# Regrouping positions by their residue of 16, and turning the dilation-16 probabilities with VectorE's 32x32 block transposes

## The chip, the core and the metric

One core of a Trainium2 chip runs the whole program in one launch. TensorE (PE; PEld is its weight load) does matmuls, VectorE (DVE) and ScalarE (ACT) the elementwise work, GpSimd (POOL) some elementwise work and the DMAs that add while they write, and SyncE (SP) issues most DMAs. The metric is the device time of one execution in microseconds, as the median of several runs.

## The reference

Two encoder layers work on 512 positions of width 1024 in float32. Each normalises x, projects it, runs two attention branches, gates both with SiLU, projects back and adds to x. Branch A is latent attention with 8 heads. Branch B is dilated attention in three groups (window, dilation): (128, 1), (512, 4) and (2048, 16), each with 8 heads of 64. Positions are gathered by stride, so that a query of group g sees only keys of its own residue class modulo the dilation:

```python
for g, (window, dil) in enumerate(DIL_PAIRS):
    ...
    o, lse = banded_attention(to_strided(q, dil), to_strided(k, dil), to_strided(v, dil),
                              window // (2 * dil))
...
alpha = jax.nn.softmax(jnp.stack(lses, axis=0), axis=0)
out = jnp.einsum('gbsh,gbshd->bshd', alpha, jnp.stack(outs, axis=0).astype(jnp.float32))
```

With 512 positions, dilation 16 has 16 classes of 32 positions, and the window of 2048 takes in each class whole. Dilation 4 has 4 classes of 128 positions and a band of 64 to either side. The three outputs of a position are weighted by their softmax denominators.

## The kernel before, in words

Activations lie with features on the 128 partitions and the 512 positions along the row. The positions do not lie in natural order: `order()` sorts them by residue of 4, so that each of the four residue classes is one block of 128 columns. Inside a block they are in ascending order. Heads are treated in pairs p = 0..3 (a = 0, 1 is the head of the pair, on 64 partitions each).

The dilated work is cut into 12 units u, each a group g and a pair p. Units 0, 1, 6, 7 have g = 0 (dilation 1, "near"), units 2, 3, 8, 9 have g = 1, and units 4, 5, 10, 11 have g = 2 (dilation 16). A unit makes q and k from a projection (`dil_qk`, which calls `rope`), then scores (`near_scores` or `far_scores`), then the product with the values (`near_out` or `far_out`).

- Near units need positions in another order than the rest, since a dilation of 1 crosses the four blocks. They are re-sorted on the way. `near_values` (L572) writes the values in chunks of 128 positions, `rope` does it for keys (L642) and for queries (L645, in two pieces of 128 and 384 columns), and `merge_rows` (L452, two pieces) puts the output back. All four are VectorE additions or products that have to run anyway. The re-sorting is in their access patterns, which have contiguous runs of 32 or 16 floats.
- The near units' running minima and sums (16 bytes per position) are re-sorted by DMAs through memory, in `by_residue`: one write (L702) and five reads (L706 to L708) per pair, on SP's queue.
- `far_scores` works per block of 128 positions for g = 1 and g = 2 alike: a 128x128 score block, a mask added by VectorE (L758), and a minimum taken by a custom instruction (L761); then ScalarE's exponential (L765). For g = 1 the mask is a band. For g = 2 it lets through a quarter of the block: keys that agree with the query modulo 4 within the block. For g = 2 the shares of the three groups follow (`shares`, L809 to L818), and POOL multiplies the probabilities by them (L773, 8 instructions of 128x128).
- `far_out` turns the probabilities, so that keys lie on partitions. `transpose_split` does it with four 128x128 transposes on TensorE into a PSUM bank (L457). ScalarE copies the bank as a rounded high part (`split`, L222), VectorE makes the low part (L223), and TensorE multiplies with the values (L793). ScalarE and VectorE add up the halves (L796, L797, L799).

Matmuls in full precision are made of three products of high and low parts, `triple` (L242 to L244). So weights are also split after loading: ScalarE copies the high part (L199), VectorE subtracts (L204), or POOL issues a DMA that adds (L202).

The order of the work is made by `Weave.run`. A main line of projections runs on, and side lines (norms, scores, outputs, combination) give pieces in between when their needs were finished a set lag ago. Each piece yields what it costs TensorE in this plan, and `LG2` is the lag between a dilation-16 unit's scores and its turning. Behind that a scheduler puts the instructions on each engine's queue, which then runs strictly in order.

## Time and profile before

| | |
|---|---|
| median of 3 runs | 933.5 us (932.68 to 936.16) |
| the profiled execution | 936.2 us |
| its span, first to last instruction | 934.4 us |
| PE busy | 910.4 us (97%) |
| DVE busy | 690.9 us (74%) |
| ACT busy | 597.8 us (64%) |
| POOL busy | 315.1 us (34%) |
| granted TensorE clock | 0.995 |

The profile is of one execution, which is 0.3% above the median. The matmuls' durations overlap (each row's mean is from its start to its modelled end), so what one of many costs is better read from the spacing of their starts. The chain of waits is followed back from the last instruction, and each of its pieces is time in which that instruction kept the end waiting. Time is in microseconds from the start of the span.

### The profile page before, as it was taken

The numbers are of one execution on the slowest core, as the hardware profiler recorded it, in microseconds if no ns is written. First come the engines' busy times: TensorE is split into PE (matmuls) and PEld (weight loads), VectorE is DVE, ScalarE is ACT, GpSimd is POOL, SyncE is SP. The second block draws the span as 40 slices with busy tenths as digits, with TensorE's granted clock in tenths as the row PEclk, the third lists the DMA queues.
The fourth block names the chain that finished last, engine by engine and source line by source line (L and its number), as shares of the span: only waits on it lengthen the run. The fifth ranks groups of instructions, "written<-read, shape, count | busy, mean of one in ns | idle before, by whom it ended". The sixth has DMA issues, their size and how long they took to land.

```text
span 934.4 us, 15835 instructions
## 1 busy us (share of the span) xinstructions
PE 910.4 (97%) x5172; PEld 775.1 (83%) x5172; DVE 690.9 (74%) x1732; ACT 597.8 (64%) x1448; POOL 315.1 (34%) x367
## 2 busy tenths in 40 slices
PE   8999999999999999999999999999999999999996
PEld 6978888988889889887897888888888888897775
DVE  6756787877868766688766578797778776757864
ACT  6546776666857766754454578666767586676533
POOL 0034253344542431333312444423554234224300
PEclk9999999999999999999999999999999999999999
DMA  7357453276554764655553854516666557366432
GB/s 272 115 121 141 105 122 68 66 161 147 122 123 93 149 131 104 136 147 147 171 155 104 163 121 86 114 46 138 139 129 148 131 101 148 84 144 144 130 123 90
DMA packets 85746, 118.66 MB, mean 127 GB/s; under 512 B 16864, under 2 KB 34848, under 8 KB 85664
## 3 DMA queue, kind: packets, MB, share of 16 engines
q1 hardware_dynamic: 65648, 81.80, 29.8%
q0 software_dynamic: 19584, 35.66, 24.2%
q8 instruction: 41, 0.67, 0.3%
q14 instruction: 41, 0.34, 0.1%
q10 hardware_dynamic: 432, 0.20, 0.1%
HBM read 113.26 MB, written 4.36 MB: 126 GB/s over the span
## 4 chain that ended last, share of the span: by engine, by line
PE 81%; DVE 8%; ACT 4%; DMA 3%; issue 3%; POOL 1%; ACTq 0%; DVEq 0%; POOLq 0%
PE bank L242 22%; PE bank L244 22%; PE bank L243 22%; PE bank L457 5%; PE bank L558 3%; PE bank L752 1%; PE bank L793 1%; PE bank L681 1%; DMA whl<-wst 1%; DVE pt L223 1%; DMA wraw<-wst 1%; ACT whl L199 1%; DVE tmp L638 1%; POOL tmp L636 1%; DVE whl L204 1%
## 5 line engine op out<-in xcount | busy, mean ns | idle before, releaser
L242 PE MATMUL bank<-hl,whl 128*128 128x512 f32 x728 | 290.2, 399 | 2.2 <-ACT hl L222 1.4
L244 PE MATMUL bank<-hl,whl 128*128 128x512 f32 x728 | 284.4, 391 | 2.0 <-DMA whl<-wst 2.0
L243 PE MATMUL bank<-hl,whl 128*128 128x512 f32 x728 | 284.5, 391 | 0.0
L199 ACT CAST whl<-wraw 128x512 fp32r<-128x512 f32 (+3 forms) x243 | 143.8, 596 | 119.4 <-PE bank L244 77.5
L202 POOL DMA_DIRECT2D whl<-wst x136 | 119.7, 889 | 223.9 <-ACT whl L201 161.5
L244 PEld LDWEIGHTS bank<-hl,whl 128*128 128x128 f32 x728 | 136.7, 188 | 32.5 <-DMA whl<-wst 2.9
L242 PEld LDWEIGHTS bank<-hl,whl 128*128 128x128 f32 x728 | 136.6, 188 | 29.2 <-ACT hl L222 1.8
L243 PEld LDWEIGHTS bank<-hl,whl 128*128 128x128 f32 x728 | 137.0, 188 | 24.6 <-DVE hl L223 0.3
L242 PE MATMUL bank<-whl,hl 128*128 128x256 f32 (+2 forms) x328 | 99.8, 304 | 1.5 <-ACT hl L222 1.5
L244 PE MATMUL bank<-whl,hl 128*128 128x256 f32 (+2 forms) x328 | 98.3, 300 | 0.0
L243 PE MATMUL bank<-whl,hl 128*128 128x256 f32 (+2 forms) x328 | 98.1, 299 | 0.0
L204 DVE TENSOR_TENSOR whl<-wraw,whl 128x512 fp32r<-128x512 f32 (+3 forms) x107 | 76.1, 717 | 26.0 <-ACT whl L199 25.0
L636 POOL TENSOR_TENSOR tmp<-tmp,sd 128x512 f32<-128x512 f32 x48 | 63.2, 1316 | 89.5 <-DVE tmp L634 65.4
L223 DVE TENSOR_TENSOR pt<-bank,pt 128x512 fp32r<-128x512 f32 x128 | 83.6, 684 | 5.6 <-ACT pt L222 4.2
L201 ACT ACTIVATE whl<-wraw 128x512 fp32r<-128x512 f32 x136 | 86.3, 635 | 0.1
L222 ACT CAST pt<-bank 128x512 fp32r<-128x512 f32 x128 | 69.9, 588 | 10.7 <-PE bank L457 10.3
L538 POOL TENSOR_SCALAR p<-p,lc 128x512 f32<-128x512 f32 x64 | 48.9, 771 | 71.4 <-DVE lc L537 70.6
L457 PE MATMUL bank<-ident,p 128*128 128x128 f32 x512 | 67.7, 275 | 0.0
L242 PEld LDWEIGHTS bank<-whl,hl 128*128 128x128 f32 x328 | 62.5, 191 | 3.9 <-ACT hl L222 1.8
L244 PEld LDWEIGHTS bank<-whl,hl 128*128 128x128 f32 x328 | 62.5, 191 | 2.0 <-DVE hl L223 0.4
L243 PEld LDWEIGHTS bank<-whl,hl 128*128 128x128 f32 x328 | 62.5, 191 | 1.7
L457 PEld LDWEIGHTS bank<-ident,p 128*128 128x128 f32 x512 | 59.2, 142 | 5.4
(178 smaller groups left out, 1612.5 us busy)
## 6 DMA issues: line engine op xcount, KB each, us to landing
wraw<-wst SPq DMA_DIRECT2D x218, 256.0 KB, 2.9
whl<-wst POOLq DMA_DIRECT2D x136, 256.0 KB, 4.5
tmp<-shd SPq DMA_DIRECT2D x32, 128.0 KB, 4.4
xl<-xT SPq DMA_DIRECT2D x10, 256.0 KB, 2.7
wraw<-wst SPq DMA_DIRECT2D x16, 144.0 KB, 2.2
wraw<-wst SPq DMA_DIRECT2D x12, 192.0 KB, 2.6
x1d<-xl SPq DMA_DIRECT2D x8, 256.0 KB, 2.9
xl<-x1d SPq DMA_DIRECT2D x8, 256.0 KB, 3.0
```

The lines of the kernel that those rows point to most:

```text
L199: nc.scalar.copy(hi, src)
L201: nc.scalar.mul(lo, src, -1.0)
L202: nc.gpsimd.dma_start(lo, wst[l * len(PLAN) + i, :, :c], accum_op=ALU.add)
L204: nc.vector.tensor_tensor(lo, src, F(hi), op=ALU.subtract)
L222: nc.scalar.copy(dst_hi, src)
L223: nc.vector.tensor_tensor(dst_lo, src, F(dst_hi), op=ALU.subtract)
L242: nc.tensor.matmul(a, w[:, 0], h[:, 0], start=first, stop=False)
L243: nc.tensor.matmul(a, w[:, 0], h[:, 1], start=False, stop=False)
L244: nc.tensor.matmul(a, w[:, 1], h[:, 0], start=False, stop=last)
L457: nc.tensor.transpose(b[:, 128 * i:128 * i + 128], x, ident)
L538: nc.gpsimd.tensor_scalar(pt, pt, l1, 0.0, op0=ALU.mult, op1=ALU.add)
L636: nc.gpsimd.tensor_tensor(u, u, L.sd, op=ALU.mult)
```

## The change

The positions inside each block of 128 get another order: first by residue of 16, then ascending. So a block is now four runs of 32 positions, one for each class of dilation 16, and a 128x128 block of dilation-16 probabilities has nonzero values only in its four 32x32 blocks on the diagonal. The mask for g = 2 changes with that, and so do the tables and the order in which x is handed over.

- In `far_out` with g = 2, VectorE's 32x32 block transpose (one instruction over the 128x512 tile, in place) stands where four TensorE transposes into a bank stood. ScalarE's copy and VectorE's subtraction now read the tile in place of the bank. The piece yields 0.0 in place of 0.9 to the weave.
- The re-sorting of the near units now goes between "block, residue of 16, ascending" and "ascending, residue". The access patterns of L572, L642, L645 and L452 take single floats at a step of 32 floats on one side; they had runs of 32 or 16 floats.
- `by_residue` writes with three DMAs (one of 128x3x4 floats, two of 64x4) in place of one, and reads with four in place of five.

```diff
-def near_chunks(x):
-    return x.rearrange("p (r c t) -> p c r t", r=4, c=4)
+def by_16(x):
+    return x.rearrange("p (m s) -> p s m", m=16)
...
     def near_values(L, p):
-        nc.vector.tensor_tensor(f.rearrange("p (c r t) -> p c r t", c=4, r=4), near_chunks(a), near_chunks(L.rb), op=ALU.mult)
+        nc.vector.tensor_tensor(f.rearrange("p (s m) -> p s m", m=16), by_16(a), by_16(L.rb), op=ALU.mult)
...
-    halfway = [(lambda f: f[:, 0:128].rearrange("p (r h t) -> p r h t", r=4, h=2),
-                lambda x: x.rearrange("p (r b t) -> p r b t", r=4, t=16)[:, :, 0:8:7]),
-               (lambda f: f[:, 128:512].rearrange("p (i r t) -> p r i t", i=3, r=4),
-                lambda x: x.rearrange("p (r t) -> p r t", r=4)[:, :, 16:112].rearrange("p r (i t) -> p r i t", i=3))]
+    halfway = [(lambda f: f[:, 0:128].rearrange("p (h s m) -> p h s m", h=2, m=16),
+                lambda x: x.rearrange("p (m b s) -> p b s m", m=16, s=4)[:, 0:8:7]),
+               (lambda f: f[:, 128:512].rearrange("p (s m) -> p s m", m=16), lambda x: by_16(x)[:, 4:28])]
...
         if order == "keys":
-            nc.vector.tensor_tensor(f.rearrange("p (c r t) -> p c r t", c=4, r=4), near_chunks(t1), near_chunks(u), op=ALU.add)
+            nc.vector.tensor_tensor(f.rearrange("p (s m) -> p s m", m=16), by_16(t1), by_16(u), op=ALU.add)
...
     def by_residue(L, p):
-        nc.sync.dma_start(sd.rearrange("(i m) x -> m i x", m=128), st)
+        nc.sync.dma_start(sd[64:448].rearrange("(i m) x -> m i x", m=128), st[:, 1:4])
+        for h in range(2):
+            nc.sync.dma_start(sd[448 * h:448 * h + 64], st[64 * h:64 * h + 64, 0])
         L.st[p] = t([128, 4, 3, 4], F32, "st", 4)
-        blocks = sd.rearrange("(i r t) x -> i t r x", i=4, r=4)
-        for i in range(3):
-            nc.sync.dma_start(L.st[p][16 + 32 * i:48 + 32 * i, :, 0], blocks[i + 1])
-        nc.sync.dma_start(L.st[p][0:16, :, 0], blocks[0, 0:16])
-        nc.sync.dma_start(L.st[p][112:128, :, 0], blocks[0, 16:32])
+        for m in range(4):
+            nc.sync.dma_start(L.st[p][32 * m:32 * m + 32, :, 0], sd.rearrange("(s r m) x -> m s r x", r=4, m=4)[m])
...
     def far_out(L, u):
             pt = L.p.pop(("d", u, rp))
-            tts.append(transpose_split([pt[:, 128 * i:128 * i + 128] for i in range(4)]))
+            if g == 2:
+                nc.vector.transpose(pt, pt)
+                tt = t([128, 2, S], FR, "pt", 2)
+                split(tt[:, 0], tt[:, 1], pt)
+                tts.append(tt)
+            else:
+                tts.append(transpose_split([pt[:, 128 * i:128 * i + 128] for i in range(4)]))
         yield ("t", L.l, "d", u)
-        yield 0.9, LG
+        yield 0.9 if g == 1 else 0.0, LG
...
 def order():
-    return np.arange(S).reshape(128, 4).T.reshape(-1)
+    return np.arange(S).reshape(32, 4, 4).transpose(2, 1, 0).reshape(-1)
```

What is left out are the masks and the tables that follow from the new order, and the shape of the mask in L758 (four rows of 32 in place of 32 rows of 4).

The scheduler places the new instructions by what they need, and not where the code stands. Three places matter below. The names carry buffer numbers, which differ between the two programs; lines from L703 on are up to 5 higher after the change.

The first place is VectorE's queue in layer 0, behind the shares of unit 10; `og` and its `tmp` belong to the unit before it, q and kst (with their `tmp`) to unit 11. Before:

```order
L797 TENSOR_TENSOR tmp_4700<-bank_4697,tmp_4700 64x2x128
L799 TENSOR_TENSOR og_4635<-bank_4697,tmp_4700 64x256
L223 TENSOR_TENSOR q_4674<-tmp_4668,q_4674 128x512
L223 TENSOR_TENSOR pt_4715<-bank_4710,pt_4715 128x512
L223 TENSOR_TENSOR pt_4723<-bank_4718,pt_4723 128x512
L634 STREAM_SHUFFLE tmp_4745<-bank_4684 128x512
L635 TENSOR_TENSOR tmp_4744<-bank_4684,cd_455 128x512
L638 TENSOR_TENSOR tmp_4744<-tmp_4744,tmp_4745 128x512
L223 TENSOR_TENSOR kst<-tmp_4744,kst 128x512
```

The same stretch after the change:

```order
L801 TENSOR_TENSOR tmp_4688<-bank_4685,tmp_4688 64x2x128
L781 STREAM_TRANSPOSE p_4556<-p_4556 128x512
L223 TENSOR_TENSOR q_4662<-tmp_4656,q_4662 128x512
L803 TENSOR_TENSOR og_4623<-bank_4685,tmp_4688 64x256
L223 TENSOR_TENSOR pt_4703<-bank_4698,pt_4703 128x512
L223 TENSOR_TENSOR pt_4711<-bank_4706,pt_4711 128x512
L633 STREAM_SHUFFLE tmp_4733<-bank_4672 128x512
L634 TENSOR_TENSOR tmp_4732<-bank_4672,cd_455 128x512
L781 STREAM_TRANSPOSE p_4583<-p_4583 128x512
L637 TENSOR_TENSOR tmp_4732<-tmp_4732,tmp_4733 128x512
L223 TENSOR_TENSOR kst<-tmp_4732,kst 128x512
```

The two transposes of unit 10 were put far ahead of the unit's output work. The first stands ahead of the low part of unit 11's q, the second between the two additions that make unit 11's k.

The second place is TensorE's queue where unit 10 was turned. Before, the turning stood between unit 11's scores and a projection:

```order
L755 MATMUL bank_4884<-kst,q_4674 128x128
L755 MATMUL bank_4885<-kst,q_4674 128x128
L457 MATMUL bank_4923<-ident,p_4568 128x128 x4
L457 MATMUL bank_4931<-ident,p_4595 128x128 x4
L242 MATMUL bank_4819<-hl_183,whl_4755 128x512
L243 MATMUL bank_4819<-hl_183,whl_4755 128x512
```

The same place after the change:

```order
L753 MATMUL bank_4872<-kst,q_4662 128x128
L753 MATMUL bank_4873<-kst,q_4662 128x128
L242 MATMUL bank_4807<-hl_183,whl_4743 128x512
L243 MATMUL bank_4807<-hl_183,whl_4743 128x512
L244 MATMUL bank_4807<-hl_183,whl_4743 128x512
```

The eight transposes are gone. All eight dilation-16 units of the two layers lose theirs, 64 in all, and the rest of TensorE's queue keeps its order but for five matmuls.

The third place is VectorE's queue at unit 10's low parts (`pt` from the turned probabilities). Before, they stood behind the minima of unit 11 (`p_4883`):

```order
L761 ISA p_4883,st_3966<-bank_4885,p_4883 128x128
L761 ISA st_3966 128x1
L223 TENSOR_TENSOR pt_4928<-bank_4923,pt_4928 128x512
L809 TENSOR_REDUCE mm_4904<-st_3966 128x8
L223 TENSOR_TENSOR pt_4936<-bank_4931,pt_4936 128x512
```

After, the first stands in front of a weight's low part (`whl`) and ahead of all of unit 11's minima (`p_4832` is its first half):

```order
L434 SCALAR_TENSOR_TENSOR gate_4786<-gate_4786,tmp_4784 128x512
L803 TENSOR_TENSOR og_4770<-bank_4789,tmp_4792 64x256
L223 TENSOR_TENSOR pt_4912<-p_4556,pt_4912 128x512
L204 TENSOR_TENSOR whl_4862<-wraw_4860,whl_4862 128x512
L756 TENSOR_TENSOR p_4832<-bank_4833,msk 128x2x128
L756 TENSOR_TENSOR p_4832<-bank_4834,msk 128x2x128
```

The second low part stands behind that first half of the minima, so both moved up on VectorE. In layer 1 the same three places look the same.

More of the change, by code (lines that the diff above doesn't have):

```diff
@@ L741, in far_scores @@
         st = L.st[p][:, :, g]
-        m = msk[:, 512:640].rearrange("p (x y) -> p x y", y=4) if g == 1 else msk[:, 640:644].unsqueeze(1).to_broadcast([128, 32, 4])
+        m = msk[:, 512:640].rearrange("p (x y) -> p x y", y=32) if g == 1 else msk[:, 640:644].unsqueeze(2).to_broadcast([128, 4, 32])
         pt = t([128, S], F32, "p", 8)
@@ L745, in far_scores @@
         banks = [bank() for _ in range(2)]
-        by4 = lambda x: x.rearrange("p j (x y) -> p j x y", y=4)
+        by4 = lambda x: x.rearrange("p j (x y) -> p j x y", y=32)
         for j in range(2):
@@ L757, in far_scores @@
             s = banks[a].rearrange("p (j l x) -> p j l x", j=2, l=2)
-            nc.vector.tensor_tensor(by4(p4[:, :, a]), by4(s[:, :, 0]), m.unsqueeze(1).to_broadcast([128, 2, 32, 4]), op=ALU.add)
+            nc.vector.tensor_tensor(by4(p4[:, :, a]), by4(s[:, :, 0]), m.unsqueeze(1).to_broadcast([128, 2, 4, 32]), op=ALU.add)
             for j in range(2):
@@ L1104, in constants @@
     tables = np.ascontiguousarray(np.stack([cd, sd, cmq, smq])[:, :, order()], np.float32)
-    near = np.arange(S).reshape(4, 32, 4).transpose(0, 2, 1).reshape(-1)
+    near = np.arange(S).reshape(32, 4, 4).transpose(0, 2, 1).reshape(-1)
     keytab = np.stack([c32, s32])[:, :, order()].reshape(2, 32, 4, 128).transpose(3, 0, 2, 1).reshape(128, 256)
@@ L1109, in constants @@
     q = near[:128, None] + 64
-    ends = np.where(near[:128, None] < 64, near[:128, None], 384 + near[:128, None])
-    i, j = np.arange(128)[:, None], np.arange(128)[None, :]
-    ok = [np.abs(q - k) <= 64, np.abs(ends - np.where(k < 128, k, 256 + k)) <= 64, np.abs(i - j) <= 64, i % 4 == j[:, :4]]
+    ends = np.concatenate([near[:64, None], near[448:, None]])
+    i = order()[:128] // 4
+    i, j = i[:, None], i[None, :]
+    ok = [np.abs(q - k) <= 64, np.abs(ends - np.where(k < 128, k, 256 + k)) <= 64, np.abs(i - j) <= 64, i % 4 == j[:, :128:32] % 4]
     masks = np.where(np.concatenate(ok, axis=1), 0.0, BIG).astype(np.float32)
```

## The prediction

> **What bounds the kernel now.** I read the page first, then the chain of waits, then single stretches of the timeline. The profiled execution took 936.2 us: a span of 934.4 and 1.8 around it.
>
> ```profile
> span 934.4 us, 15835 instructions
> PE 910.4 (97%) x5172; PEld 775.1 (83%) x5172; DVE 690.9 (74%) x1732; ACT 597.8 (64%) x1448; POOL 315.1 (34%) x367
> ...
> PE 81%; DVE 8%; ACT 4%; DMA 3%; issue 3%; POOL 1%; ACTq 0%; DVEq 0%; POOLq 0%
> ```
>
> TensorE is busy 97% of the span and carries 81% of the chain, so work taken off it shortens the run, except in the stretches where the chain runs through VectorE, ScalarE or a DMA. There TensorE would only wait longer. The chain shows three such stretches that lie on the changed units. At the end of layer 0, around unit 11's scores:
>
> ```profile
> 393.70 0.68 ACT p L765 x4
> ...
> 400.10 0.90 DVE q L223
> ...
> 422.77 0.73 PE bank L242 x2
> ```
>
> From 393.7 to 422.8 nearly every link is VectorE's, one instruction behind the other. At the end of layer 1 the chain comes in over a DMA instead, joins VectorE at 866.9, and later goes over weights:
>
> ```profile
> 857.25 6.15 DMA whl<-wst
> ...
> 866.95 0.69 DVE whl L204
> ...
> 873.10 0.60 DVE pt L223
> ...
> 878.94 0.50 PE bank L242
> ...
> 890.96 4.26 DMA wraw<-wst
> ...
> 904.30 0.47 PE bank L793 x2
> ```
>
> **TensorE's 64 transposes.** They lie in eight groups of eight, one for each dilation-16 unit. Where a group stands on the chain it costs 0.87 us, as in the first and the last of five such groups (units 4, 5 and 11 of layer 0, units 4 and 5 of layer 1):
>
> ```profile
> 234.52 0.88 PE bank L457 x8
> ...
> 738.99 0.87 PE bank L457 x8
> ```
>
> The other three lie in the stretches above, two beside unit 11's scores and one in the tail of layer 1:
>
> ```profile
> 412.96 1.09 PE L457 MATMUL bank<-ident,p 128*128 128x128 f32 x8
> 869.23 1.09 PE L457 MATMUL bank<-ident,p 128*128 128x128 f32 x8
> 892.83 1.03 PE L457 MATMUL bank<-ident,p 128*128 128x128 f32 x8
> ```
>
> All eight would give 8 x 0.87 = 7.0 us. I count the five on the chain, **-4.4 us**, and nothing for the three, since there TensorE waits for others at 422.8, 878.9 and 904.3. The bounds are -4.4 and -7.0. The mean of 275 ns that the by-form groups give for one of these transposes is not their price, because they overlap:
>
> ```profile
> L457 PE MATMUL bank<-ident,p 128*128 128x128 f32 x512 | 67.7, 275 | 0.0
> L634 DVE STREAM_SHUFFLE tmp<-bank 128x512 f32<-128x512 f32 x48 | 35.7, 744 | 0.1
> L223 DVE TENSOR_TENSOR pt<-bank,pt 128x512 fp32r<-128x512 f32 x128 | 83.6, 684 | 5.6 <-ACT pt L222 4.2
> ```
>
> **VectorE's 16 block transposes.** No row shows one. The nearest is the shuffle of a 128x512 tile, which also moves data across partitions: 744 ns. I take 0.75 us, so VectorE gains 16 x 0.75 = 12 us of work. The bounds are nothing (if they fit into idle time everywhere) and twice the row, 1.5 us. VectorE has 934.4 - 690.9 = 243 us idle, so what counts is where they land. In the five groups on TensorE's chain I cost them at nothing: VectorE's idle time and the plan's lags hide them, and if that cover were gone each pair would cost up to its 1.5 us. The first place is VectorE's queue of layer 0 at 399.6, with what GpSimd does at that time:
>
> ```profile
> 399.18 0.43 DVE L797 TENSOR_TENSOR tmp<-bank,tmp 64x256 f32<-64x256 f32 x1
> 399.64 0.43 DVE L799 TENSOR_TENSOR og<-bank,tmp 64x256 f32<-64x256 f32 x1
> 404.46 0.69 DVE L638 TENSOR_TENSOR tmp<-tmp,tmp 128x512 f32<-128x512 f32 x1 [0.92 <-POOL tmp L636]
> 398.35 3.59 POOL L773 TENSOR_SCALAR p<-p,e 128x128 f32<-128x128 f32 x8
> ```
>
> The first transpose needs GpSimd's first four share products, which end about half way through the eight, at 398.35 + 1.80 = 400.15. It comes up at 399.62, waits 0.5, runs 0.75, and q's low part, then k and everything behind them start 1.05 to 1.25 later; I take **+1.1 us**. The second comes where VectorE waits 0.92 us for GpSimd and fits. Were it 1.5 us long, both would cost 0.75 + 0.6 more. In layer 1 the same delay ends in the idle 0.83 us ahead of the weight at 866.95, since the chain there comes over the DMA:
>
> ```profile
> 866.95 0.69 DVE L204 TENSOR_TENSOR whl<-wraw,whl 128x512 fp32r<-128x512 f32 x1 [0.83 <-ACT whl L199]
> ```
>
> Unit 11's own transposes fall, in layer 0, between weight splits that wait for ScalarE and, in layer 1, into the 1.23 and 0.60 us shown here:
>
> ```profile
> 429.41 0.69 DVE L204 TENSOR_TENSOR hl<-wraw,hl 128x512 fp32r<-128x512 f32 x1 [0.76 <-ACT hl L199]
> 430.73 0.69 DVE L204 TENSOR_TENSOR hl<-wraw,hl 128x512 fp32r<-128x512 f32 x1 [0.63 <-ACT hl L199]
> 887.75 1.39 DVE L204 TENSOR_TENSOR whl<-wraw,whl 128x512 fp32r<-128x512 f32 x2 [1.23 <-ACT whl L199]
> 892.98 0.69 DVE L839 TENSOR_TENSOR og<-og,tmp 128x512 f32<-128x512 f32 x1 [0.60 <-DMA tmp<-shd]
> ```
>
> I cost them at nothing; at 1.5 us each they would overfill these gaps by about 1 us in each layer.
>
> **The low parts that move up.** The copy and the subtraction read the tile in place of a bank, at the same price, I assume: both engines handle such tiles all the time. In layer 1 the first low part moves into the 0.83 us at 866.1 and leaves the chain, where it stood with 0.60 at 873.10: **-0.6 us**. In layer 0 there is no gap at its new place, and nothing is won. Bounds: 0 and -1.2.
>
> **The re-sorting at a step of 32 floats.** It touches VectorE only. These are the groups, each for all eight near units (L645 and L452 have a second piece of 128 columns, and L452 runs once for each head):
>
> ```profile
> L642 DVE TENSOR_TENSOR tmp<-tmp,tmp 128x512 f32<-128x512 f32 x8 | 5.5, 689 | 4.2 <-POOL tmp L636 4.2
> L572 DVE TENSOR_TENSOR tmp<-bank,rb 128x512 f32<-128x512 f32 x8 | 5.5, 684 | 3.8 <-PE bank L244 3.8
> L452 DVE TENSOR_TENSOR og<-bank,tmp 64x384 f32<-64x384 f32 x16 | 8.8, 547 | 0.0
> L452 DVE TENSOR_TENSOR og<-bank,tmp 64x128 f32<-64x128 f32 x16 | 4.6, 287 | 4.4 <-ACT tmp L450 4.3
> ```
>
> So five passes over 512 columns for a near unit: one for values, one for keys, one for queries, two for outputs. They run at (547 - 287)/256 = 1.02 ns per column, with runs of 16 to 32 floats. The trace has no wide operation at a step above one float. The nearest rows are two tiny reductions over 24 floats: L809 steps by four floats, L816 by two.
>
> ```profile
> L809 DVE TENSOR_REDUCE mm<-st 128x8 f32<-128x24 f32 x8 | 1.4, 177 | 0.1
> L816 DVE TENSOR_REDUCE ls<-el 128x8 f32<-128x24 f32 x8 | 1.3, 166 | 0.0
> ```
>
> The wider step costs 11 ns for 24 floats, 0.46 ns per float, so 0.23 us for a pass of 512. The bounds are 0 and a doubled pass, 0.52. On the chain stand six of these passes, the first and the last being:
>
> ```profile
> 93.50 0.68 DVE tmp L642
> ...
> 587.30 0.77 DVE og L452 x2
> ```
>
> 6 x 0.23 = **+1.4 us**, between 0 and 3.1. The other 34 passes lie beside TensorE's work and add 34 x 0.23 = 8 us to VectorE's; without that cover they would count in full.
>
> **The sums' DMAs and the weave.** A pair issues three writes and four reads in place of one and five. I cost this at nothing. The reads go out when all writes have landed, as before with one, and SP's weight loads queue behind them; the consumers come a unit later. If a write landed a microsecond late, the weights behind it would, eight times in the run. The mask keeps its number of elements.
>
> **The sum**: -4.4 + 1.1 - 0.6 + 1.4 = **-2.5 us**. That makes 936.2 - 2.5 = 933.7 for the profiled execution, and 933.5 - 2.5 = **931.0** for the median.
>
> **Rivals.** *Everything comes through* (faster). All eight groups count, the block transposes and the steps cost nothing on the path: -7.0 - 0.6 = -7.6, so 925.9. For it: TensorE's 97%, and that a block transpose takes no PSUM bank, so waits of TensorE such as that at 904.3 could go too. Against it: VectorE has hardly any idle time between 395 and 422. Half way there already passes -4.7, by which I call it faster.
>
> *The step of 32 floats takes over* (slower). Its place are the near units 0 and 1 of both layers, where the chain already passes L642 and L452. If a pass doubles (+0.52) and VectorE's slack there is used up, all their passes come onto the path: 4 units x 5 passes x 0.52 = 10.4, and the sum is -4.4 + 1.1 - 0.6 + 10.4 = +6.5, so 940.0. It decides from (4.7 + 3.9)/20 = 0.43 us per pass, 0.84 ns per column. For it: L809 against L816 points this way. Against it: that difference is half of what is needed, and most of the 40 passes stand beside TensorE's work. [...]
>
> *A block transpose is twice as long* as the shuffle: +1.35 at 400, and about 1 in each layer behind unit 11, makes -2.5 + 3.35 = +0.9, so 934.4. This stays within no change.
>
> **Chances.** What a measurement here can tell from no change is about 0.5%, 4.7 us. My forecast and its neighbours (the long transpose, a free or a middling step) get 0.58 for within that, the first rival and half ways to it 0.28, the second 0.14. The range goes from near the first rival, 926.0, to where a step at its upper bound on the present chain and a long transpose together lead (931.0 + 1.7 + 3.35 = 936.1), and a little into the second rival: 937.5.
>
> **What would show it.** Right: L457 at 448 on the page, eight fewer groups on TensorE; a transpose row near 750 ns; VectorE's busy time up by some 20 us (12 and 40 x 0.23); a wait of VectorE for GpSimd ahead of the transpose near 400; the wait at 422.8 longer than before. L642 at 0.92 against 0.69 would confirm the step's price; 0.69 would mean that it is free and the sum near -3.9, 1.2 a doubled pass. I would be wrong if TensorE's waits between 58 and 140, or 515 and 596, grew by several microseconds, or if DVE left the chain between 395 and 422.

## The result, and the profile after

| | before | after |
|---|---|---|
| median | 934.8 us (932.7 to 937.8, 4 runs) | 943.3 us (942.3 to 944.0, 4 runs) |
| ratio, 95% interval | | 1.0093 [1.0067, 1.0118] |
| the profiled execution | 936.2 us | 943.3 us |
| its granted TensorE clock | 0.995 | 0.987 |

The median before is now of four runs; the 933.5 above was of the first three. The change makes the kernel slower by 0.9%. The forecast was 931.0, inside 926.0 to 937.5. The page of the kernel after:

```profile
span 941.6 us, 15703 instructions
...
PE 908.7 (97%) x5108; PEld 772.2 (82%) x5108; DVE 716.8 (76%) x1748; ACT 597.2 (63%) x1448; POOL 311.5 (33%) x367
...
PE 78%; DVE 10%; ACT 4%; DMA 3%; issue 3%; POOL 2%; ACTq 0%; DVEq 0%; POOLq 0%; SPq 0%
```

TensorE has 64 matmuls fewer, but its busy time falls by only 1.7 us, and VectorE's rises by 26. The chain moved from TensorE (81 to 78%) to VectorE (8 to 10%). The groups of the kernel after, by form (L641 was L642):

```profile
L781 DVE STREAM_TRANSPOSE p<-p 128x512 f32<-128x512 f32 x16 | 11.3, 708 | 3.6 <-POOL p L771 3.6
L641 DVE TENSOR_TENSOR tmp<-tmp,tmp 128x512 f32<-128x512 f32 x8 | 9.8, 1225 | 4.3 <-POOL tmp L635 4.3
L572 DVE TENSOR_TENSOR tmp<-bank,rb 128x512 f32<-128x512 f32 x8 | 8.9, 1108 | 1.2 <-PE bank L244 1.2
L452 DVE TENSOR_TENSOR og<-bank,tmp 64x384 f32<-64x384 f32 x16 | 14.1, 880 | 0.0
L452 DVE TENSOR_TENSOR og<-bank,tmp 64x128 f32<-64x128 f32 x16 | 6.2, 390 | 4.4 <-ACT tmp L450 4.3
L457 PE MATMUL bank<-ident,p 128*128 128x128 f32 x448 | 60.3, 278 | 0.0
```

A block transpose takes 708 ns, where I took 750. The keys' pass went from 689 to 1225 ns and the values' from 684 to 1108: plus 0.54 and 0.42 us, where I took 0.23. An output's two pieces went from 547 + 287 to 880 + 390, plus 0.44.

TensorE's own long waits, from its timeline after (in brackets the idle time and what ended it):

```profile
423.89 0.72 PE L242 MATMUL bank<-hl,whl 128*128 128x512 f32 x2 [3.07 <-ACT hl L222]
...
885.94 0.79 PE L242 MATMUL bank<-whl,hl 128*128 128x512 f32 x1 [2.75 <-ACT hl L222]
...
911.57 0.47 PE L797 MATMUL bank<-pt,v 128*128 128x256 f32 x2 [2.68 <-DVE og L803]
```

The same products before:

```profile
422.77 0.73 PE L242 MATMUL bank<-hl,whl 128*128 128x512 f32 x2 [1.38 <-ACT hl L222]
...
878.94 0.50 PE L242 MATMUL bank<-whl,hl 128*128 128x512 f32 x1 [1.54 <-ACT hl L222]
...
904.30 0.47 PE L793 MATMUL bank<-pt,v 128*128 128x256 f32 x2 [1.51 <-DVE og L799]
```

Behind the first two waits after the change stands something that I had not put into the sum at all. Windows of the kernel after, with TensorE's granted clock (PEclk) behind the five engines:

```profile
421.00:424.00 3.00, 0.11 (x1) 0.11 (x1) 3.00 (x8) 1.50 (x4) 1.02 (x1) 1.00 0.00 0
425.20:428.50 3.30, 3.30 (x9) 2.65 (x8) 2.69 (x5) 1.14 (x2) 3.30 (x6) 0.50 0.36 107
...
886.00:889.30 3.30, 3.30 (x10) 2.72 (x11) 3.24 (x9) 1.66 (x4) 2.26 (x5) 0.50 0.47 130
```

The same window of the kernel before:

```profile
425.20:428.50 3.30, 3.30 (x18) 2.76 (x17) 2.83 (x5) 1.79 (x5) 2.79 (x6) 1.00 0.66 174
```

Soon behind such a wait TensorE runs for 3.4 us at half clock: 9 matmuls in 3.3 us, where before there were 18. One such stretch costs up to 1.7 us (an estimate: half of its length). After has six of them (at 8.7, 138.4, 425.1, 595.8, 776.7 and 885.9), before two (136.2 and 880.3), besides one at the end of each. They don't follow every wait, nor long ones alone: none stands behind the wait of 2.68 us that ends at 911.6, and those at 138.4 and 595.8 stand behind waits of which the longest are 0.80 and 0.81 us. Within each profile their starts lie whole multiples of 3.413 us apart (84 between 138.4 and 425.1, 50 between 425.1 and 595.8), and this grid lies elsewhere in each profile. So it is partly chance which wait gets one. Averaged over all runs of a kernel, (1 - clock) x time says how much the clock took: 2 to 3 us before, 10.6 after.

What the prediction named as proof of its steps: L457 is at 448; VectorE's busy time rose by 26 and not by 20 us; it waits for GpSimd ahead of the first transpose of unit 10 (row below); the wait at 422.8 is longer. Idle time of TensorE around units 0 and 1 also grew: 0.85 to 1.17 us near 110, and in layer 1 a new wait of 0.96 near 568. That was the sign of the second rival.

```profile
400.85 0.71 DVE L781 STREAM_TRANSPOSE p<-p 128x512 f32<-128x512 f32 x1 [0.53 <-POOL p L771]
```

In the two stretches that the prediction named for this sign, TensorE's busy time fell from 80.15 to 78.64 us and from 80.00 to 78.29, so its idle time grew by 1.5 and 1.7 us. First before, then after (TensorE's busy time stands behind the length):

```profile
58.00:140.00 82.00, 80.15 (x447) 67.34 (x446) 59.62 (x146) 57.41 (x136) 36.10 (x37) 0.98 0.60 124
515.00:596.00 81.00, 80.00 (x454) 67.32 (x453) 59.81 (x149) 57.67 (x137) 35.72 (x37) 1.00 0.62 125
```

```profile
58.00:140.00 82.00, 78.64 (x437) 66.13 (x436) 62.39 (x142) 55.37 (x127) 36.04 (x37) 0.99 0.59 122
515.00:596.00 81.00, 78.29 (x435) 65.67 (x434) 61.83 (x141) 54.69 (x126) 35.18 (x36) 1.00 0.58 125
```

### The profile page after: what moved, and what is told of

The parts are those of the page before. It is cut to its first block, busy times and chain, and to the rows that moved or that the text cites. A ratio compares the mean times of both kernels' runs of the same rounds, so it can differ in the third digit from the quotient of the medians.

```text
span 941.6 us, 15703 instructions
## 1 busy us (share of the span) xinstructions
PE 908.7 (97%) x5108; PEld 772.2 (82%) x5108; DVE 716.8 (76%) x1748; ACT 597.2 (63%) x1448; POOL 311.5 (33%) x367
## 4 chain that ended last, share of the span: by engine, by line
PE 78%; DVE 10%; ACT 4%; DMA 3%; issue 3%; POOL 2%; ACTq 0%; DVEq 0%; POOLq 0%; SPq 0%
PE bank L242 22%; PE bank L243 21%; PE bank L244 21%; PE bank L457 4%; PE bank L558 3%; DMA wraw<-wst 2%; PE bank L750 1%; DVE pt L223 1%; PE bank L797 1%; PE bank L680 1%; POOL tmp L635 1%; DVE whl L204 1%; DVE og L452 1%; DMA whl<-wst 1%; ACT p L536 1%
## 5 line engine op out<-in xcount | busy, mean ns | idle before, releaser
L223 DVE TENSOR_TENSOR pt<-bank,pt 128x512 fp32r<-128x512 f32 x112 | 73.0, 683 | 4.1 <-ACT pt L222 2.7
L222 ACT CAST pt<-bank 128x512 fp32r<-128x512 f32 x112 | 61.1, 587 | 6.1 <-PE bank L457 5.7
L763 ACT ACTIVATE p<-p,st 128x128 f32<-128x128 f32 x128 | 50.0, 393 | 18.0 <-DVE st L759 17.9
L457 PE MATMUL bank<-ident,p 128*128 128x128 f32 x448 | 60.3, 278 | 0.0
```

What stands on the lines that cost most here:

```text
L222: nc.scalar.copy(dst_hi, src)
L223: nc.vector.tensor_tensor(dst_lo, src, F(dst_hi), op=ALU.subtract)
L457: nc.tensor.transpose(b[:, 128 * i:128 * i + 128], x, ident)
L763: nc.scalar.activation(p4[:, j, a], p4[:, j, a], AF.Exp, scale=-1.0, bias=st[:, b, a:a + 1], accum_out=st[:, b, 2 + a:3 + a])
```

## The experiments

All times are medians; each ratio is to the kernel before on the same chip, with its 95% interval. "Clock" is the mean granted TensorE clock of a kernel's runs; before had 0.996 to 0.998. The kernels ran on several chips, so two of them are compared by their ratios to before; "give or take" is the uncertainty of such a difference, from both intervals. Where the text follows TensorE's products from one profile to another, it speaks of one execution of each kernel.

| kernel | what it is | us | ratio | clock |
|---|---|---|---|---|
| after | the change | 943.3 | 1.0093 [1.0067, 1.0118] | 0.989 |
| e1 | the order without the turn | 940.7 | 1.0069 [1.0053, 1.0086] | 0.994 |
| e2 | the turn without the order | 937.3 | 1.0027 [1.0008, 1.0047] | 0.992 |
| e3 | the change, passes with before's runs | 937.4 | 1.0034 [1.0015, 1.0052] | 0.992 |
| e4 | the change, zeros in four waits | 939.8 | 1.0055 [1.0033, 1.0076] | 0.994 |
| e5 | the change, turned early only | 935.2 | 1.0010 [0.9992, 1.0029] | 0.994 |
| e7 | the change, keys and values in runs of 8 | 941.9 | 1.0079 [1.0056, 1.0102] | 0.989 |
| e8 | e5, all passes in runs of 2, 8 reads of the sums | 939.2 | 1.0034 [1.0016, 1.0052] | 0.993 |
| e9 | e8, zeros in six waits | 942.6 | 1.0071 [1.0052, 1.0090] | 0.991 |
| e10 | e8, MLA output emitted earlier | 943.4 | 1.0081 [1.0060, 1.0103] | 0.991 |
| e11 | e5, all passes in runs of 2, 4 reads | 931.5 | 0.9964 [0.9946, 0.9982] | 0.996 |
| e12 | e5, early transposes three times over | 936.4 | 1.0017 [0.9998, 1.0035] | 0.996 |
| e13 | the change, late transposes three times over | 945.0 | 1.0114 [1.0077, 1.0150] | 0.988 |
| e14 | e8, the 8 reads on GpSimd's queue | 932.2 | 0.9975 [0.9956, 0.9994] | 0.993 |
| e15 | e14, zeros at the start and at unit 2 | 929.3 | 0.9932 [0.9913, 0.9951] | 0.997 |
| e16 | e14, turned late too | 936.4 | 1.0017 [1.0000, 1.0034] | 0.991 |
| e17 | e16, zeros in the layer-end waits | 939.1 | 1.0034 [1.0014, 1.0054] | 0.993 |

MLA is branch A, the latent attention. "Early" means units 4 and 5 of both layers, "late" units 10 and 11, which stand at the layers' ends. e6 ran once, so it has no interval and is not in the table.

### The two parts apart: e1, e2, e3

e1 takes the block transposes back out of the change; e2 puts them into the kernel before, whose order doesn't fit them; e3 is the change with before's access patterns in the re-sorting passes, so that near units see positions in another order.

```diff
 e1, in far_out
-            if g == 2:
-                nc.vector.transpose(pt, pt)
...
+            tts.append(transpose_split([pt[:, 128 * i:128 * i + 128] for i in range(4)]))
 e3, as in before: near_values, rope, halfway
-            nc.vector.tensor_tensor(f.rearrange("p (s m) -> p s m", m=16), by_16(t1), by_16(u), op=ALU.add)
+            nc.vector.tensor_tensor(f.rearrange("p (c r t) -> p c r t", c=4, r=4), near_chunks(t1), near_chunks(u), op=ALU.add)
```

> The changed kernel with its new order of positions, its steps of 32 floats and its DMAs, but the dilation-16 probabilities turned by TensorE again, as before. Theory A (the steps of 32 floats double VectorE's re-sorting passes, TensorE waits longer at the near units, and the block transposes are a gain): the 64 transposes come back (about +7 us) and the steps stay, so slower than the changed kernel: 945 to 950 us, 1.2 to 1.7% over the kernel before; TensorE's waits near 110, 136 and 594 as in the changed kernel, the wait at 424 shorter than 3.07. Theory B (the block transposes and their place in VectorE's queue cost the time, the steps are hidden): the loss goes, 935 to 938 us. Theory C (the three writes and four reads of the sums hold up the weights): 941 to 950 us, and the wait for weights near 776 stays at 2.6.

> The kernel before with its order of positions, runs and DMAs, and only the dilation-16 turning done by VectorE's block transposes. Its probabilities are not block-diagonal in that order, so that what it sums for dilation 16 is another sum of the same size. Theory A: the gain without the price, 927 to 930 us (0.5 to 0.8% faster than before), with L452, L642, L572 and L645 at the durations of before. Theory B: 939 to 943 us. Theory C: as A.

> The changed kernel, DMAs of the sums included, but with the re-sorting passes of the near units in the old patterns with runs of 16 and 32 floats (so the near units see their positions in a wrong order). Theory A: as the turning alone, 927 to 931 us, and TensorE's waits at the near units back to before (0.85 near 109, none over 0.6 near 135 and 590). Theory B: 939 to 943 us. Theory C: 937 to 943 us, so clearly slower than the turning alone.

The order alone costs 0.7%. The turn alone, with 64 matmuls less on an engine that is 97% busy, is no gain either but 0.3% slower. So the theory that steps of 32 floats eat up a gain was half right: there was no gain to eat. e3 has the change's own DMAs and e2 those of before, and they differ by 0.07%, give or take 0.27%: a cost of three writes and four reads in place of one and five doesn't show, but up to 3 us of it could hide here.

### What a step costs: e6

```diff
-            nc.vector.tensor_tensor(f.rearrange("p (s m) -> p s m", m=16), by_16(t1), by_16(u), op=ALU.add)
+            nc.vector.tensor_tensor(steps(L, p, f, False), steps(L, p, t1), steps(L, p, u), op=ALU.add)
```

> The change, with the keys' addition (two inputs in SBUF) and the values' multiplication (one in PSUM, one in SBUF) read at another step in each pair: in layer 0 single floats at steps of 2, 4, 8 and 16 floats, in layer 1 a step of 32 floats with runs of 1, 2, 4 and 8 floats (near units see keys in a wrong order). [...] Rival B (only the step of 32 floats, 128 bytes, is bad): 4 to 16 floats near 689, runs of 2 already halve the extra.

The keys' addition in this kernel's timeline of VectorE, first the pairs of layer 0 (steps of 2, 4, 8, 16 floats), then of layer 1 (runs of 1, 2, 4, 8 floats at a step of 32):

```profile
65.16 0.69 DVE L648 TENSOR_TENSOR tmp<-tmp,tmp 128x512 f32<-128x512 f32 x1 [0.92 <-POOL tmp L642]
...
93.49 1.06 DVE L648 TENSOR_TENSOR tmp<-tmp,tmp 128x512 f32<-128x512 f32 x1
...
263.59 1.24 DVE L648 TENSOR_TENSOR tmp<-tmp,tmp 128x512 f32<-128x512 f32 x1 [0.74 <-POOL tmp L642]
...
328.77 1.11 DVE L648 TENSOR_TENSOR tmp<-tmp,tmp 128x512 f32<-128x512 f32 x1 [0.85 <-POOL tmp L642]
...
523.83 1.22 DVE L648 TENSOR_TENSOR tmp<-tmp,tmp 128x512 f32<-128x512 f32 x1 [0.91 <-POOL tmp L642]
...
552.12 0.69 DVE L648 TENSOR_TENSOR tmp<-tmp,tmp 128x512 f32<-128x512 f32 x1
...
721.09 0.69 DVE L648 TENSOR_TENSOR tmp<-tmp,tmp 128x512 f32<-128x512 f32 x1
...
792.04 0.69 DVE L648 TENSOR_TENSOR tmp<-tmp,tmp 128x512 f32<-128x512 f32 x1 [0.85 <-POOL tmp L642]
```

A step of 2 floats is free, 4 costs 54% and 8 to 32 cost 60 to 80%. What counts is not the step's length alone: two floats read side by side make the step of 32 free. Rival B fails: steps of 4 to 16 floats, which it had near 689 ns, took 1.06 to 1.24 us, and runs of 2 took away the whole extra and not half of it. The change could have had its order without the price.

### Turned early only: e5, and the doubled transposes: e12, e13

```diff
 e5
-            if g == 2:
+            if g == 2 and p < 2:
...
-        yield 0.9 if g == 1 else 0.0, LG
+        yield 0.9 if g == 1 or p > 1 else 0.0, LG
 e12 (on e5, p < 2) and e13 (on the change, p > 1)
-                nc.vector.transpose(pt, pt)
+                for _ in range(3 if p < 2 else 1):
+                    nc.vector.transpose(pt, pt)
```

> The change, with VectorE turning P only in units 4 and 5 of both layers; units 10 and 11, at the layer ends, go back to TensorE. Theory L (turning pays wherever TensorE is the bound, and costs at the layer ends, where VectorE is): the waits near 422 and 885 fall back to 1.4 and 1.6 us with no half clock behind them, and the time is that of the order alone less 4 x 0.87: 940.7 - 3.5 = 937. Rival V (block transposes cost through VectorE's load wherever they stand): half of the turning's loss stays, 941 to 943.

> Block transposes in units 4 and 5 alone, each done three times over (which gives the same as once): 2 x 0.71 x 2 = 2.8 us more of VectorE's time in each of four units. Theory L (there VectorE's time is hidden behind TensorE): within 1 us of 935.2. Rival V (VectorE's load costs everywhere): 4 x 2.8 = 11 us more, 946.

> The change, with the block transposes of units 10 and 11 alone done three times over: again 2.8 us more of VectorE's time in each of four units. Theory L (at the layer ends VectorE's time is on the path): the four units add most of 11 us, to 950 or more, and the waits near 424 and 886 grow by 2 to 3 us each. Rival K (what costs there is the clock, not VectorE's time): 943 to 945.

Theory L held for e5, more strongly than expected. From e1 to e5 four groups of eight matmuls go and with them 0.59% (1.0069 to 1.0010), 5.5 us, give or take 2.3. From e5 to the change the other four go, and 0.83% come back, 7.8 us, give or take 3. TensorE's waits at the layer ends in e5:

```profile
423.06 0.73 PE L242 MATMUL bank<-hl,whl 128*128 128x512 f32 x2 [1.28 <-ACT hl L222]
...
879.90 0.50 PE L242 MATMUL bank<-whl,hl 128*128 128x512 f32 x1 [1.53 <-ACT hl L222]
...
903.07 0.47 PE L797 MATMUL bank<-pt,v 128*128 128x256 f32 x2 [0.88 <-DVE og L803]
```

They are at or below what they were before (1.38, 1.54 and 1.51). e12 confirms the other half: 11 us more of VectorE's time in the early units costs 0.7 us, inside the uncertainty. But e13 goes against the theory's wording. The same 11 us more in the late units cost 2 us (1.0093 to 1.0114, give or take 4) and not most of 11. At that rate the 5.7 us that the late transposes take in the change would explain 1 us of the 7.8, and at the upper end of the uncertainty 3. So their duration is not the main part of what the late turn costs.

### Zeros in the waits: e4, e9, e15, e17

If the half clock behind a wait is what costs, TensorE can be kept busy in the wait with products that add zero to a bank:

```diff
+    zero = const.tile([128, 128], FR, name="zero")
+    def fill(a, h, n, start=False):
+        for _ in range(n):
+            nc.tensor.matmul(a, zero, h, start=start, stop=start)
 e4, e9, e17: before the last MLA chunk of the first output at both layer ends
+            if (n, k) == (0, 3):
+                fill(a, ms[0][:, 0], 11)
 e9, e15: around unit 2's scores
+            if first:
+                fill(banks[0][:, 0:256], L.h[0][:, 0, 0:256], 3, True)
```

e4, e9 and e17 also emit the three outputs' last MLA chunks behind their first three, so that the real work stands ahead of the zeros. So these three differ from the kernels without zeros by that order too.

> The change, with products by a tile of zeros (they add nothing to any sum) in four places where TensorE waits: 6 more before the first product of the program, 9 ahead of the weight that is late near 776, 11 and 10 ahead of the last MLA chunk at the two layer ends (near 424 and 886). The waits themselves are not shortened. Theory K (half of the loss is the clock: a long wait of TensorE is followed by 3.4 us at half clock, about 1.7 us each): the half-clock stretches near 9, 425, 777 and 886 go, those near 138 and 596 stay; the mean clock rises from 0.988 to about 0.994 and the time falls by 4 x 1.7 = 6 to 7 us, to about 937. Rival W (the waits cost themselves and no more; the clock falls by chance): the time stays at 943, or grows by what the zeros take beyond the waits.

> The kernel with both corrections, and zeros in TensorE's waits again, cut to the shorter waits (4 more products at the start, 4 and 5 ahead of the layer-end waits, 8 ahead of the late weight near 775, and 9 of 256 columns around unit 2's scores in both layers). Theory K (clock): against the kernel without them the clock rises to 0.998 and 2 to 3 us go. Rival W: the same time within 1 us.

> The kernel of 932.2 (block transposes early, runs of 2, the reads on GpSimd's queue) with 4 more products at the start and 9 products of 256 columns by zeros around unit 2's scores in both layers, inside waits of 1.1, 1.6 and 2.8 us. Theory K (half clock follows such waits and costs): the half-clock stretches near 134 and 588 go and the time falls by 1 to 3 us, to 929 to 931. Rival W: 932 or more, since the products are late for the waits and add to them.

> The kernel with late block transposes too, and zeros (11 and 10 products) in the waits ahead of the last MLA chunk at both layer ends, which keeps the clock up there. Theory K (the late turn's cost is the half clock behind these waits): it comes down to 932 to 934. Rival Q (VectorE's queue, with the transposes and GpSimd's products ahead of them, sets when the stretch ends, whatever the clock): it stays within 1.5 us of the kernel without the zeros.

In the profiled execution of e4 all six half-clock stretches of the change are gone, and one came at 904.8, behind a wait that had no zeros. In e9 and e17, too, none stands at the filled places, so it is TensorE's idle time that brings it on (e16 and e17 below: a granted clock of 0.50 and of 1.00 in the same window). It is not the whole account: the two near 138 and 596 went in e4 without zeros, and in e15 one near 589 stayed in spite of them. And the time fell by 3.6 us and not by 6 to 7. The starts of the same products in both traces say where: 1.1 us were won at the start and 1.8 at the late weight near 777, and 1.6 and 1.4 near 138 and 596, while 1.1 were lost near 110. But at the layer end of 392 to 455, where the change loses 2.3 us against before, e4 still loses 2.0, and behind 904 it gives back 2.4. In e17 theory K fails as a forecast: 1.0034 with zeros against 1.0017 without, give or take 0.26%, where 932 to 934 us were expected. TensorE's waits in e16 (turned late, no zeros):

```profile
421.12 1.19 PE L247 MATMUL bank<-hl,whl 128*128 128x512 f32 x2 [2.59 <-ACT hl L227]
...
904.37 0.47 PE L803 MATMUL bank<-pt,v 128*128 128x256 f32 x2 [2.86 <-DVE og L809]
```

The same places in e17:

```profile
421.44 0.50 PE L256 MATMUL bank<-hl,whl 128*128 128x512 f32 x1 [0.39 <-DVE hl L236]
...
428.68 0.47 PE L255 MATMUL bank<-hl,whl 128*128 128x512 f32 x1 [1.56 <-ACT tmp L814]
...
904.27 0.48 PE L811 MATMUL bank<-pt,v 128*128 128x256 f32 x2 [3.66 <-DVE og L817]
```

And the clock behind the first wait, in a window of e16 and in one of e17:

```profile
421.20:424.50 3.30, 3.30 (x8) 2.65 (x9) 2.10 (x7) 1.23 (x3) 2.28 (x5) 0.50 0.42 102
```

```profile
421.20:424.50 3.30, 3.06 (x16) 2.66 (x17) 2.31 (x7) 0.83 (x2) 2.84 (x8) 1.00 0.53 151
```

The clock stays up in e17, TensorE does twice the matmuls in that window, and then it waits 1.56 us at 428.7 and 0.8 us longer at 904. By the starts of the same products, the stretch of 392 to 455 loses 2.6 us from e14 to e16 and still 2.0 from e14 to e17, which has no half clock there. So most of what TensorE wins it hands back at the next wait, which ScalarE and VectorE end; the other order of the MLA chunks may have a part in that. At the end of layer 1 e17 is no test of the theory: its half clock came at 905.3 in place of 878.6, and the mean clock of its runs is only 0.993 against 0.991. Where TensorE itself is the bound, the clock seems to cost: e15 has zeros only at the start and around unit 2, and goes from 0.9975 to 0.9932, give or take 0.27%, with the clock from 0.993 to 0.997. The two profiled executions don't show it: each has two half-clock stretches besides the one at its end (e14 at 134.0 and 588.0, e15 at 589.1 and 875.8), and e15's is the longer by 1.6 us. e9 is the miss of this set: against e8 it won 1.7 us at the start and 1.6 near 777, but it lost 1.6 at the end of layer 0, where e8 has no half clock to avoid, it has new half-clock stretches at 568.8 and 910.1, behind waits without zeros, and it takes 0.4% more in the end.

### The passes against the queue of the sums: e7, e8, e11, e14

```diff
 e8, e11, e14: near order by groups of 32, then residue, then two ascending
+def by_16(x):
+    return x.rearrange("p (m g s) -> p g m s", m=16, s=2)
+def pairs(f):
+    return f.rearrange("p (g m s) -> p g m s", m=16, s=2)
 e8: the sums' reads, one for each residue and parity
+            for s in range(2):
+                nc.sync.dma_start(L.st[p][32 * m + s:32 * m + 32:2, :, 0],
+                                  sd.rearrange("(g r m s) x -> m s g r x", r=4, m=4, s=2)[m, s])
 e14
-                nc.sync.dma_start(
+                nc.gpsimd.dma_start(
```

> The change, with the near units' keys and values ordered within their blocks of 128 by residue of 16 first, so that these two of the five passes read runs of 8 floats; masks to match, queries and outputs as in the change. Theory A (the steps cost what the order costs): the two passes fall to about 690 ns, 2 of 5 passes are won back where they stand on the chain (near units 0 and 1), and the time falls by 2 to 4 us to 939 to 941. Rival D (the order costs by its DMAs): no change from 943.

> The change with two corrections: VectorE turns P only in units 4 and 5, and the near units' tokens are ordered within groups of 32 so that all five passes read or write runs of 2 floats (8 small reads of the sums in place of 4, two small pieces for the queries' ends in place of one). Theory A (the doubled passes are what the order costs): the passes fall to 0.69 us, and from 935.2 go the 3 us of the order's extra waiting and some clock: 931 to 933. Rival D (most of the order's cost is something else, as the small gain of the keys' and values' runs hints): 934 to 935.

> Block transposes in units 4 and 5 alone, and all five re-sorting passes in runs of 2 floats, with the change's own 3 writes and 4 reads of the sums (so the sums come in a wrong order; the queues do the same work as in the change). Theory A (the doubled passes are the order's cost): against 935.2 with doubled passes 2 to 4 us go, to 931 to 933. Rival D (the order's cost is its DMAs on SyncE's queue, which hold the weights): no change, 935, and only the 8 reads of the earlier kernel made 939.

> Block transposes in units 4 and 5 alone, passes in runs of 2 floats, and the 8 reads of the sums issued by GpSimd in place of SyncE. Theory S (the 8 reads held SyncE's weight loads, and that made 939): the wait of ScalarE for a weight near 100 falls from 6.1 us to about 2.3, and the time to 931 to 934. Rival G (GpSimd waits for the sums in its turn and holds the low parts of the weights): 937 or more.

e7 came out 1.4 us faster by two of the five passes, which is inside the uncertainty (give or take 3 us). e8 should have won 3 us and lost 4 instead. Its trace shows why: ScalarE waits for a weight. The row of e8, and the same weight in the change:

```profile
103.92 0.62 ACT L204 CAST whl<-wraw 128x512 fp32r<-128x512 f32 x1 [6.09 <-DMA wraw<-wst]
```

```profile
100.45 0.62 ACT L199 CAST whl<-wraw 128x512 fp32r<-128x512 f32 x1 [2.41 <-DMA wraw<-wst]
```

The reads of the sums stand on SyncE's queue ahead of that weight's load. A read takes SyncE about 0.6 us to issue (median 0.597 in the change, L706), and four more of them, behind the wait for the writes, made the weight 3.7 us later. So I split the two: e11 keeps cheap passes and goes back to four reads, e14 keeps the eight and takes them off SyncE's queue. Both come out faster than before. From e5 to e11 only the passes' access patterns differ: 1.0010 to 0.9964, 0.46% or 4.3 us, give or take 2.4. That is the price of the doubled passes, and theory A holds. From e8 to e14 only the queue of the eight reads differs: 1.0034 to 0.9975, 5.5 us, give or take 2.4. In e14's profile TensorE's waits near 110 and for the weight near 770 are gone; the kernel before had 0.85 and 1.39 us there.

### The late turn by itself: e16, and the queue: e10

e16 differs from e14 by `if g == 2` in place of `if g == 2 and p < 2`, with the yield that goes with it. e10 gives the MLA outputs a line of their own in the weave (on e8).

> The kernel of 932.2 with block transposes in units 10 and 11 too, so that only this differs. If the late turn costs in itself, as between the kernels of 935.2 and 943.3: 938 to 940. If it cost only together with the doubled passes: 930 to 933, by the four groups that leave TensorE.

> The kernel with both corrections, and the MLA output of pair 3 emitted in a line of its own, so that its gate product stands about 65 instructions earlier in VectorE's queue, ahead of unit 11's scores. Theory Q (the layer-end waits are VectorE's queue ahead of that product): the waits of 1.3 and 1.5 us near 422 and 880 go, and with them 2 to 3 us. Rival R: VectorE is the bound of the whole stretch; the waits come back some microseconds later, at unit 10's and 11's outputs, and the time stays.

The late turn costs by itself: 0.9975 to 1.0017, 0.42% or 3.9 us, give or take 2.4, although 32 matmuls go that were worth 3.5 us elsewhere. VectorE's queue at the end of layer 1 in e16 shows what TensorE waits for there. Rows of its timeline:

```profile
899.10 0.69 DVE L209 TENSOR_TENSOR whl<-wraw,whl 128x512 fp32r<-128x512 f32 x1 [2.12 <-ACT whl L204]
901.53 1.33 DVE L209 TENSOR_TENSOR whl<-wraw,whl 128x512 fp32r<-128x512 f32 x2 [1.74 <-ACT whl L204]
902.90 0.88 DVE L807 TENSOR_TENSOR tmp<-bank,tmp 64x256 f32<-64x256 f32 x2
903.80 0.88 DVE L809 TENSOR_TENSOR og<-bank,tmp 64x256 f32<-64x256 f32 x2
```

The additions that free TensorE's banks (L809, for which TensorE waits at 904.37) are not late because VectorE is busy. They stand behind weights for which VectorE itself waits 2.12 and 1.74 us, in the order that the scheduler gave. ScalarE makes these weights' high parts. It waited for a block transpose first and then for the weight's load:

```profile
892.71 0.62 ACT L227 CAST pt<-p 128x512 fp32r<-128x512 f32 x1 [3.17 <-DVE p L787]
...
898.45 0.62 ACT L204 CAST whl<-wraw 128x512 fp32r<-128x512 f32 x1 [2.54 <-DMA wraw<-wst]
```

Whether the first of these waits makes the second isn't shown. In e14 VectorE's longest wait for such a weight there is 1.17:

```profile
892.52 0.69 DVE L209 TENSOR_TENSOR whl<-wraw,whl 128x512 fp32r<-128x512 f32 x1 [1.17 <-ACT whl L204]
```

e10 is a miss. The MLA product moved up, the wait near 422 went, and waits of 1.6 us near 438 and 1.05 near 444 came in its place: rival R, and 0.5% more.

## Why the prediction was wrong, point by point

- **The five groups on TensorE's chain, -4.4.** Right for the four early ones: they gave 5.5 us against 4 x 0.87 = 3.5, and the two ratios' intervals allow the difference; by the starts of the same products in the profiles before and after they gave 3.7. The fifth, unit 11's of layer 0, gave nothing: it lies in the stretch of the layer's end, where 2.3 us were lost in all.
- **Nothing for the other three, and +1.1 for the first block transpose near 400.** This is the first step that failed. The transpose near 400 did what I had worked out (0.53 us of waiting, 0.71 of running, the second one all but hidden), but I closed the sum there. Turning late costs 3.9 us by itself (e14 to e16) and 7.8 together with the doubled passes (e5 to the change). I took relief on TensorE in these stretches as worth zero at worst. It was worth less than that: the queues behind were put in another order, TensorE ran into longer waits (3.07 us for 1.38 at 423.9), and in e16 VectorE's own waits stand ahead of the additions that free TensorE's banks. In the profiles before and after, the whole loss of these stretches lies at the end of layer 0: 2.3 us, where I had 1.1 - 0.9 = 0.2. Only 0.4 of it is there when TensorE goes on at 423.9, the rest comes behind, with the half clock at 425.1. The end of layer 1 came 0.25 us shorter.
- **Six passes on the chain by 0.23, +1.4.** The second step that failed, and by size: a pass costs 0.42 to 0.54 more, and all of them together 4.3 us (e5 to e11), against bounds of 0 and 3.1. In the profiles before and after, units 0 and 1 lose 1.7 us in layer 0 and 3.5 in layer 1, the latter with the new half clock at 595.8. The row that I scaled from (L809 against L816, 24 floats) was no measure for a wide operation: after the change it still reads 178 against 164 ns. The second rival had the right price, 0.52. It had the place half right too: 4.3 of its 10.4 us came onto the path.
- **The low parts that move up, -0.6.** It did not come. The chain of the kernel after still goes over the low part at the end of layer 1, and over the block transpose too:

```profile
862.89 0.71 DVE p L781
...
874.43 0.69 DVE pt L223
```

- **The sums' DMAs at nothing.** Not refuted for three writes and four reads (e3 against e2, with room for 3 us); eight reads on that queue cost 5.5 us. But a term near them is missing: TensorE's wait for a weight near 770 grew from 1.39 to 2.57 us, with a new half clock behind it, 2.8 us in all. On the chain that weight's transfer, issued by GpSimd, is longer by 1.2 us, first before and then after:

```profile
764.59 5.37 DMA whl<-wst
```

```profile
769.15 6.58 DMA whl<-wst
```

  The wait varies in the other kernels with three writes and four reads (2.18 in e5, 3.17 in e1, 3.72 in e11) and is gone in e14. What makes the transfer longer stays open.
- **What was missing.** Half clock behind long waits. By the clocks of all runs it grew by 8 us; where TensorE is the bound it seems to cost (4.0 us from e14 to e15), at the end of layer 0 most of it stands inside time that is lost anyway (e17).

For the two profiled executions the account closes. Against before, the products after run late by 0.8 us from the start, 5.2 at units 0 and 1, 2.3 at the end of layer 0 and 2.8 at the weight near 770; 3.7 are won at units 4 and 5 and 0.25 at the end of layer 1. That is the 7.1 us by which the span grew. I take the 0.8 for luck: it comes from TensorE's second wait of the program, near 6 us, which no edit but the zeros touches, and which was anything from 1.00 (e6) to 2.68 us (e3).

What stays open: over the experiments the single steps don't add up. The turn alone would be a gain by its two measured halves (-5.5 and +3.9), and it measured +0.3% in e2; the early turn on the old order was not run. Half-clock stretches come or go with small shifts of the waits and with the place of the 3.413 us grid, which is a difference of up to 1.7 us each, and I haven't separated that for each kernel. Nor is it settled why the order alone costs 0.7% when its doubled passes explain 0.46%; e8 and e14 point to SyncE's queue, e3 against e2 does not.

The best version is e15, 0.7% faster than before: block transposes where TensorE is the bound, passes that read two floats side by side, the reads of the sums off the queue of the weights, and zeros in three of TensorE's waits.

## What to carry to other kernels

Before work is moved off the busiest engine, split the run into stretches by which wait ends last, and take the relief only where that engine is the bound: the same edit gave 5.5 us in four units and cost 3.9 in the four others. A strided pass has to be priced by its step and by how many elements it reads side by side: single floats at a step of 32 took 1.22 us here and two side by side 0.69 (e6), as runs of 32 did before. Small DMAs are to be priced by what stands behind them on their queue: eight reads ahead of weights cost 5.5 us (e8 to e14).

## What the runs showed of the hardware

- Reading 512 columns of float32 from SBUF with VectorE (the keys' addition, 128x512) takes 0.69 us with runs of 32 floats (the kernel before, L642); in e6 it takes 0.69 at a step of 2 floats, 1.06 at 4, 1.24 at 8, 1.11 at 16, 1.22 at 32, and 0.69 at a step of 32 with two, four or eight floats side by side.
- VectorE's 32x32 block transpose of a 128x512 float32 tile in place takes 708 ns (L781 after the change, mean of 16).
- TensorE's half clock comes in stretches of 3.413 us (in the profiles before and after, but for the last of each, which runs past the span's end) behind waits (in the change's profile the longest wait just ahead of one was between 0.80 and 3.07 us), but not behind every wait: 2.68 us (the change, at 911.6) had none. Within each of these two profiles the stretches start on one grid of 3.413 us. Ten full-clock windows of that grid in the two had half clock behind them, and TensorE was idle in them for 1.00 to 3.41 us; in those without, for 1.77 us at most, so that between 1.00 and 1.77 both happened. The grid divided the wait of 2.68 us into windows with 0.92 and 1.77 us, and it passed. In e16, half clock stood behind a wait of 2.59 us (at 421.1).
- SyncE takes about 0.6 us to issue one DMA of 32 x 4 pieces of 16 bytes (L706 in the change: median 0.597 of 32, 0.539 to 1.465).
